# Opening a conditioned decoder layer in other groups of row blocks, with the later conditioning in half rows

## The chip, the cores and the metric

The kernel runs on one core of one Trainium2 chip. The metric is the device time of one execution in microseconds (us); lower is better. The median of three runs stands for a kernel. Beside them one execution was recorded by the hardware profiler; its rows are quoted here and below. Engines are named as in the profile: PE (matmuls), PEld (loads of the stationary operand), DVE (vector), ACT (scalar), POOL (GpSimd), SP (the queue that issues most of the transfers from memory, "DMA").

## The reference, cut to what matters

One layer, 256 tokens, width 2048, everything in float32. A vector `c` conditions all of it: nine vectors of 2048 (shift, scale and gate for each of three sub-layers) come from one product with a large matrix, and the first sub-layer cannot start without its shift and scale.

```python
c_act = jax.nn.silu(c)
mod = (c_act @ w_ada[l] + b_ada[l]).reshape(b, N_MOD, D_MODEL)   # w_ada: 2048 x 18432
h = modulate(rms_norm(x, norm_ffn1[l]), mod[:, 0], mod[:, 1])    # h * (1 + scale) + shift
x = x + 0.5 * mod[:, 2] * swiglu(h, w_ffn1_gu[l], w_ffn1_down[l])
h = modulate(rms_norm(x, norm_mix[l]), mod[:, 3], mod[:, 4])
x = x + mod[:, 5] * token_mixing(h, w_in[l], ...)
h = modulate(rms_norm(x, norm_ffn2[l]), mod[:, 6], mod[:, 7])
x = x + 0.5 * mod[:, 8] * swiglu(h, w_ffn2_gu[l], w_ffn2_down[l])
return rms_norm(x, norm_final)                                   # after the (one) layer
# swiglu: gate, up = split(h @ w_gu); (silu(gate) * up) @ w_down; w_gu is 2048 x 11264
```

## The kernel before, in words

**A product in three parts.** Each matrix product is made from float32 operands that are split into a high part and a rest: ACT casts a weight piece to its high part (`wh`, line 375), DVE subtracts it from the piece and leaves the rest (`wl`, line 377), and PE adds up three products (line 360): high by high (`wh,hh`), high weight by the rest of the activation (`wh,hl`), rest of the weight by high (`wl,hh`). A piece is two row blocks of 128 rows by 512 columns; with the two halves of the tokens it is 2 x 2 x 3 = 12 matmuls of 128x512. The pool `wsp` has three buffers, so ACT can cast a piece only when PE is through with the `wh` products of the piece three earlier. The loads of whole weights go into the pool `raws` (four buffers of 1 MB).

**Conditioning.** The matrix `w_ada` lies transposed in memory. One row of it here is a tile (m, k) of 128x2048 (1 MB): the 128 values k of vector m. A pass (`ada_pass`, line 220) multiplies a part of such a row with silu(c) on DVE and sums it up: a quarter, half or the whole of a row per pass.

**The opening.** The first feed-forward product needs scale (m = 1) and shift (m = 0) for every row block k of its 16, that is 32 rows, 32 MB. So its first 16 column chunks of 512 (8 of the gate, 8 of the up half; `EARLY = 8`) are computed in groups of row blocks: while PE visits all 16 chunks with the row blocks of one group, DVE conditions the row blocks of the next group. The groups are set by `bounds`. Blocks 0 and 1 come in before the groups, with two chunks in whole float32 (line 1099). For each chunk (`visit`) the sum so far has to be carried over from group to group: after a visit ACT copies the two PSUM banks `pa` out to a `part` tile (`to_parts`, line 1219), and before the next visit of that chunk ACT copies the part back into two fresh banks (`open_banks`, line 1191), on which PE adds ("seeding"; the last two chunks of a group stay in PSUM and open the next group). There are four such banks, enough for two visits. In the last group nothing is seeded: `swiglu_up` (lines 705, 706 and 710) adds the parts to the banks on DVE and multiplies gate and up.

**What else fills the opening.** From the group before the last on, the conditioning of the later vectors (`conditioning`, `ROWS_FFN1`) runs beside the products at a rate of one quarter pass per piece (`tick`), 48 passes in the third group and 16 in the last. Its rows go to one half of a slot that the rows of the groups share (`ring`, `alone`), later to buffers of `raws`, and after the opening to a slot with two places of a full row (`two_rows`). The normalised and modulated activations of a pair of row blocks come either from PE transposes (`turned_x`, row blocks under `TURNED`) or from a transposed copy of x that POOL scales (`normed_columns`); ACT modulates them (line 628) and casts them (line 636), DVE subtracts (line 637). The result of the gated chunks is turned over by DMA in steps (`later`, `turn_step`), one step per visit in the last group.

**Order.** The instructions of PE, DVE and ACT are put in order by a scheduler when the program is built, from the order in the code and a model of its own; `tc.issue_after` pins single ones. SP keeps the order of the code. At run time each engine works strictly through its own list, so an instruction that waits holds back all behind it on its engine.

Of the kernel before, what the change touches and what calls it, by code (L numbers as in the profile page):

```python
# [77 lines left out]
def layer_kernel(  # L78
# [138 lines left out]
    def ada_pass(k, w, sums, q, passes=AQ):  # L217

        at = slice(q * D // passes, (q + 1) * D // passes)
        nc.vector.tensor_tensor_reduce(  # L220
            out=w[:, at],
            in0=w[:, at],
            in1=cact[:, at],
            scale=1.0,
            scalar=0.0,
            op0=ALU.mult,
            op1=ALU.add,
            accum_out=sums[:, k, q : q + 1],
        )
# [36 lines left out]
    def conditioning(outputs, place, behind):  # L266
# [4 lines left out]
        step = 0  # L271
        for m, gain, row in outputs:
            sums = own_sums.pop() if own_sums else ada_sums()
            for k in range(KD):
                for q in range(AQ):
                    for i in range(step // AQ, min((step + pace["ahead"]) // AQ + 1, len(tiles))):
                        if i not in held:
                            held[i] = place()
                            ada_load(*tiles[i], held[i])
                    if behind is not None and step < 2 * AQ:  # L280
                        with tc.issue_after(behind.ins):
                            ada_pass(k, held[step // AQ], sums, q)
                    else:
                        ada_pass(k, held[step // AQ], sums, q)
# [348 lines left out]
    def parts_of_h(held, k, h):  # L633

        h = h.rearrange("p (k s) -> p k s", s=S)
        nc.scalar.copy(held.hi[:, k : k + 2, :], h)
        nc.vector.tensor_sub(held.lo[:, k : k + 2, :], h, held.hi[:, k : k + 2, :].bitcast(F32))
# [326 lines left out]
    tiles = [slot(), part[0]]  # L964
    ring = [tiles[0][:, :D], tiles[0][:, D:]]
# [13 lines left out]
    rows_of, alone = {}, [False]  # L979

    def place(m, k):
        if k < 1:
            rows_of[m, k] = raw_row()
        else:
            if not alone[0]:
                ring.reverse()
# [39 lines left out]
    def turned_x(k0):  # L1026

        xn = [t512()[:, : 2 * P] for _ in range(NT)]
        for t in range(NT):
            nc.scalar.mul(xn[t], x_sb[:, t, k0 * P : (k0 + 2) * P], r[:, t : t + 1])  # L1030
        turned = [bank()[:, :S] for _ in range(2)]
        for i in range(2):
# [6 lines left out]
    TURNED = 6  # L1039
# [15 lines left out]
    def normed_columns(k0):  # L1055

        xt = t512()
        both = xt.rearrange("p (k s) -> p k s", s=S)
        nc.sync.dma_start(both, x_t[k0 : k0 + 2].rearrange("k p s -> p k s"))
        nc.gpsimd.tensor_tensor(  # L1060
            out=both, in0=both, in1=root_row[0][:, None, :].broadcast_to([P, 2, S]), op=ALU.mult
        )
        return [xt[:, i * S : (i + 1) * S] for i in range(2)]

    def group(ks, passes=2):

        for k0 in ks[::2]:
            srcs = normed_columns(k0) if k0 >= TURNED else None
            for k in (k0, k0 + 1):
# [699 lines left out]
```

## Time and profile before

| | before |
|---|---|
| median of 3 runs (lowest to highest) | 2356.58 us (2356.07 to 2357.05) |
| the profiled execution | 2357.64 us, its span 2355.5 us |
| PE busy | 2335.7 us (99%) |
| DVE busy | 1673.1 us (71%) |
| ACT busy | 1367.2 us (58%) |
| moved by DMA | 630.24 MB, mean 268 GB/s |
| mean granted PE clock | 0.999 |

The span runs from the first to the last instruction of the profiled execution; what lies around it makes up the rest of its time. "Busy" is the union of an engine's instructions. Matmuls overlap each other in the records, so a group's "mean" is longer than the distance from one matmul to the next. In the timelines a row is a run of like instructions: start, length, engine, line, and in square brackets the idle time before it with what ended it.

### The profile page before, as it was taken

The page shows a single profiled execution, that of the slowest core. Times are in us where ns is not written, and L with a number is a line of the kernel's source. Part 1 is how long each engine was busy: PE and PEld are TensorE (multiplying, and loading weights), DVE is VectorE, ACT ScalarE, POOL GpSimd, SP SyncE. Part 2 cuts the span into 40 slices and gives each one's busy share as a digit, 9 for nine tenths or more (in the row PEclk, how much of TensorE's full clock was granted, in tenths as well). Part 3 has the DMA queues.
Part 4 walks back from the last instruction along what each step waited for, and adds up shares of the span by engine and source line. Part 5 has one row for each costly group of instructions (what it writes and reads, how often), then busy time and mean ns, then how long its engine had stood idle before and what let it go on. Part 6 is the DMA issues. An engine that isn't in the chain of part 4 may idle for free.

```text
span 2355.5 us, 28357 instructions
## 1 busy us (share of the span) xinstructions
PE 2335.7 (99%) x10445; PEld 1918.6 (81%) x10445; DVE 1673.1 (71%) x2576; ACT 1367.2 (58%) x1888; POOL 18.3 (1%) x27
## 2 busy tenths in 40 slices
PE   8999999999999999999999999999999999999998
PEld 5888888888888888778888888888888888888887
DVE  7788888778867768976777776676555555555656
ACT  6766567455556567774556564465455454455544
POOL 0000000000000000000000000000000000000000
PEclk9999999999999999999999999999999999999999
DMA  9989889988765889876778787754767768666553
GB/s 383 375 323 361 355 294 328 336 306 293 302 237 220 293 267 255 258 212 254 267 273 306 288 310 281 272 204 179 259 237 256 242 239 268 223 231 202 193 197 125
DMA packets 191901, 630.24 MB, mean 268 GB/s; under 512 B 113105, under 2 KB 114769, under 8 KB 121233
## 3 DMA queue, kind: packets, MB, share of 16 engines
q1 hardware_dynamic: 189266, 617.41, 74.6%
q0 software_dynamic: 1600, 9.83, 1.0%
q8 instruction: 82, 1.34, 0.2%
q10 hardware_dynamic: 896, 1.19, 0.1%
q14 instruction: 57, 0.47, 0.1%
HBM read 598.47 MB, written 4.22 MB: 256 GB/s over the span
## 4 chain that ended last, share of the span: by engine, by line
PE 96%; DMA 2%; DVE 1%; ACT 1%; issue 0%; SPq 0%; DVEq 0%; ACTq 0%
PE pa L360 93%; DMA raw<-in_w_ffn_gu_dram 1%; DMA rows_x<-in_w_ada_dram 1%; PE ps L1453 0%; DVE slot L220 0%; PE pd L1369 0%; DVE wl L377 0%; ACT wh L375 0%; DMA x_sb<-in_x_dram 0%; PE ps L360 0%; PE pa L1099 0%; PE ps L895 0%; PE pd L1099 0%; DVE rows_x L220 0%; PE ps L1369 0%
## 5 line engine op out<-in xcount | busy, mean ns | idle before, releaser
L377 DVE TENSOR_TENSOR wl<-raw,wh 128x1024 fp32r<-128x1024 f32 x792 | 963.5, 1225 | 511.0 <-ACT wh L375 451.6
L375 ACT CAST wh<-raw 128x1024 fp32r<-128x1024 f32 x792 | 830.6, 1054 | 818.7 <-PE pa L360 752.6
L360 PE MATMUL pa<-wh,hh 128*128 128x512 f32 x2184 | 597.0, 391 | 3.0 <-ACT wh L375 1.7
L360 PE MATMUL pa<-wh,hl 128*128 128x512 f32 x2184 | 592.6, 389 | 0.0
L360 PE MATMUL pa<-wl,hh 128*128 128x512 f32 x2184 | 586.2, 390 | 0.2
L360 PEld LDWEIGHTS pa<-wh,hh 128*128 128x128 f32 x2184 | 407.5, 188 | 91.6 <-ACT wh L375 2.9
L360 PEld LDWEIGHTS pa<-wl,hh 128*128 128x128 f32 x2184 | 409.4, 188 | 86.7 <-DVE wl L377 1.0
L360 PEld LDWEIGHTS pa<-wh,hl 128*128 128x128 f32 x2184 | 409.8, 188 | 86.1 <-issue 0.4
L360 PE MATMUL pa<-wh,a 128*128 128x512 f32 x1824 | 452.1, 389 | 0.0
L360 PEld LDWEIGHTS pa<-wh,a 128*128 128x128 f32 x1824 | 341.7, 188 | 70.6
L360 PE MATMUL pa<-wl,a 128*128 128x512 f32 x912 | 245.1, 389 | 0.0
L220 DVE CUSTOM_DVE_ANT_0 slot<-slot,cact 128x512 f32<-128x512 f32 (+2 forms) x288 | 219.3, 812 | 30.0 <-DMA slot<-in_w_ada_dram 29.5
L360 PEld LDWEIGHTS pa<-wl,a 128*128 128x128 f32 x912 | 171.1, 188 | 35.4
L551 ACT COPY slot<-back 128x512 uint16<-128x512 uint16 x148 | 98.7, 766 | 0.0
L220 DVE CUSTOM_DVE_ANT_0 rows_x<-rows_x,cact 128x512 f32<-128x512 f32 x124 | 78.7, 686 | 18.0 <-DMA rows_x<-in_w_ada_dram 17.8
L410 ACT CAST a<-slot 128x512 fp32r<-128x512 f32 x114 | 70.6, 620 | 29.3 <-PE pa L360 29.0
L535 ACT COPY flat<-t 128x512 uint16<-128x512 uint16 x136 | 76.7, 617 | 8.9 <-DVE t L1526 5.7
L411 DVE TENSOR_TENSOR a<-slot,a 128x512 fp32r<-128x512 f32 x114 | 77.8, 684 | 0.3 <-ACT a L410 0.3
L220 DVE CUSTOM_DVE_ANT_0 raw<-raw,cact 128x512 f32<-128x512 f32 (+1 forms) x92 | 60.7, 709 | 14.6 <-DMA raw<-in_w_ada_dram 14.5
L1219 ACT COPY slot<-pa 128x512 f32<-128x512 f32 x72 | 38.6, 589 | 21.2 <-PE pa L360 21.0
L360 PE MATMUL pa<-wh,home 128*128 128x512 f32 x160 | 39.5, 389 | 0.0
L220 DVE DVE_READ_ACCUMULATOR2_ANT sums<- 128x1 f32 x440 | 35.9, 82 | 0.0
(232 smaller groups left out, 1087.0 us busy)
## 6 DMA issues: line engine op xcount, KB each, us to landing
raw<-in_w_ffn_gu_dram SPq DMA_DIRECT2D x160, 1024.0 KB, 5.5
raw<-in_w_in_dram SPq DMA_DIRECT2D x104, 1024.0 KB, 5.8
raw<-in_w_ffn_down_dram SPq DMA_DIRECT2D x88, 1024.0 KB, 4.9
slot<-in_w_ada_dram SPq DMA_DIRECT2D x87, 1024.0 KB, 7.4
rows_x<-in_w_ada_dram SPq DMA_DIRECT2D x31, 1024.0 KB, 7.1
raw<-in_w_ada_dram SPq DMA_DIRECT2D x22, 1024.0 KB, 5.7
raw<-in_w_swa_branch_dram SPq DMA_DIRECT2D x16, 1024.0 KB, 5.0
raw<-in_w_ret_branch_dram SPq DMA_DIRECT2D x16, 1024.0 KB, 5.4
```

The costliest lines, as they stand in the source:

```text
L220: nc.vector.tensor_tensor_reduce(out=w[:, at], in0=w[:, at], in1=cact[:, at], scale=1.0, scalar=0.0, op0=ALU.mult, op1=ALU.add, accum_out= ...
L360: product = nc.tensor.matmul(banks[t], act[:, j, t * P : (t + 1) * P], weights[:, j, :], start=starts and i == 0 and j == 0, stop=ends and ...
L375: cast.append(nc.scalar.copy(hi, src).ins)
L377: low.append(nc.vector.tensor_sub(lo, src, hi.bitcast(F32)).ins)
L410: nc.scalar.copy(hi, v)
L411: nc.vector.tensor_sub(lo, v, hi.bitcast(F32))
L535: nc.scalar.copy(planes[:, i, :], words(src)[:, :, i])
L551: nc.scalar.copy(into[:, :, :, i], held["turned"][:, i])
L1219: nc.scalar.copy(p, b)
```

## The change

The opening is cut into groups of 2, 3, 4 and 7 row blocks (`bounds = (0, 2, 5, 9, 16)`, before 2, 4, 6 and 4). An odd group ends in a piece of one row block (6 matmuls). `turned_x`, `normed_columns`, `parts_of_h` and `group` take one block or two, and `TURNED` goes from 6 to 5. The rows of the groups get a slot of their own (`rows_home`); `tiles`, the result of the gated chunks, now lies on two of the three `part` slots instead. The conditioning of the later vectors starts with the last group: its 64 passes of the opening are one per piece there (16 visits of four pieces). `two_rows` has four places of half a row, `conditioning` asks for half rows (512 KB) four passes ahead, and this holds for the rest of the kernel. In the second group every third chunk (`by_vector`: 4, 7, 10, 13; chunk 1 is still in PSUM) is not seeded: it starts on fresh banks and DVE adds them to the part afterwards (line 1243 of the changed kernel). In the last group the turning also makes a step in the middle of a visit.

```diff
-    def ada_pass(k, w, sums, q, passes=AQ):
-        at = slice(q * D // passes, (q + 1) * D // passes)
+    def ada_pass(k, w, sums, q, passes=AQ, first=0):
+        n = D // passes
+        at = slice(q * n, (q + 1) * n)
+        here = w[:, (q - first) * n : (q + 1 - first) * n]
...
-        turn = [both[:, :D], both[:, D:]]
+        turn = [both[:, i * D // 2 : (i + 1) * D // 2] for i in range(4)]
...
+        def ask(at):
+            (m, k), q = tiles[at // AQ], at % AQ
+            w = place()
+            n = min(w.shape[1] * AQ // D, AQ - q)
+            w = w[:, : n * D // AQ]
+            c0 = q * D // AQ
+            nc.sync.dma_start(
+                w, w_ada[(m * KD + k) * P : (m * KD + k + 1) * P, c0 : c0 + n * D // AQ]
+            )
+            for i in range(n):
+                held[at + i] = (w, q)
+            return n
...
-                    for i in range(step // AQ, min((step + pace["ahead"]) // AQ + 1, len(tiles))):
-                        if i not in held:
-                            held[i] = place()
-                            ada_load(*tiles[i], held[i])
+                    while asked <= step + pace["ahead"] and asked < AQ * len(tiles):
+                        asked += ask(asked)
+                    w, first = held.pop(step)
...
-    tiles = [slot(), part[0]]
-    ring = [tiles[0][:, :D], tiles[0][:, D:]]
+    tiles = part[:2]
+    rows_home = slot()
+    ring = [rows_home[:, :D], rows_home[:, D:]]
...
-    TURNED = 6
+    TURNED = 5
...
-    bounds = (0, 2, 6, 12, 16)
+    bounds = (0, 2, 5, 9, 16)
...
     def open_banks(n, sums):
         seeded = sums and n in moved
+        if seeded and n in by_vector:
+            added.add(n)
+            seeded = False
...
-        for make, part in prepared.pop(n):
+        for i, (make, part) in enumerate(prepared.pop(n)):
+            if ticks and i == KB // 2:
+                turn_step()
...
     def to_parts(n):
         for p, b in zip(part_of(n), banks.pop(n)):
+            if n in added:
+                with tc.issue_after(low[-1]):
+                    nc.vector.tensor_add(p, p, b)
+                continue
             with tc.issue_after(cast[-1]):
                 nc.scalar.copy(p, b)
...
-        if g == len(groups) - 2:
-            set_pace(ROWS_FFN1, 192, place_early, 0)
+        by_vector = chunks[1::3] if g == 1 else ()
         if final:
-            pace["rate"], pace["ahead"] = 1.0, 1
+            row_ring.append(two_rows(rows_home))
+            set_pace(ROWS_FFN1, 192, place_row, AQ)
...
-            visit(n, ks, n not in stay, g == len(groups) - 2 or final and i < 8, final or (g == len(groups) - 2 and n in stay))
+            visit(n, ks, n not in stay, final, final or (g == len(groups) - 2 and n in stay))
...
-    row_ring.append(two_rows())
```

In the rows of the program's order that follow, `wh_x<-raw_y` is the cast of a piece, `slot<-pa` and `back<-pa` copy a bank out, `pa<-slot` seeds a bank; the last number of a name tells tiles apart.

The first place is the list of ACT in the first group, around the modulation of blocks 2 and 3 (`t<-ps,modc`). Before:

```order
L1219 COPY slot_6_115<-pa_72_353 128x512
L1219 COPY slot_6_115<-pa_73_354 128x512
L628 ACTIVATE t_86_420<-ps_89_425,modc_106 128x256
L628 ACTIVATE t_86_420<-ps_90_426,modc_106 128x256
L1030 ACTIVATE t_122_579<-x_sb_97,rs2_21_150 128x256
L1030 ACTIVATE t_123_580<-x_sb_97,rs2_21_150 128x256
L375 CAST wh_84_401<-raw_81_397 128x1024
L636 CAST hh_3_112<-t_86_420 128x512
L1219 COPY slot_6_115<-pa_77_377 128x512
L1219 COPY slot_6_115<-pa_78_378 128x512
L375 CAST wh_94_443<-raw_91_439 128x1024
```

And in the changed kernel:

```order
L1246 COPY slot_6_115<-pa_82_397 128x512
L1246 COPY slot_6_115<-pa_83_398 128x512
L644 ACTIVATE t_96_464<-ps_99_469,modc_106 128x256
L644 ACTIVATE t_96_464<-ps_100_470,modc_106 128x256
L1047 ACTIVATE t_122_575<-x_sb_97,rs2_21_150 128x128
L1047 ACTIVATE t_123_576<-x_sb_97,rs2_21_150 128x128
L391 CAST wh_94_445<-raw_91_441 128x1024
L653 CAST hh_3_112<-t_96_464 128x512
L1246 COPY slot_6_115<-pa_87_421 128x512
L1246 COPY slot_6_115<-pa_88_422 128x512
L391 CAST wh_104_487<-raw_101_483 128x1024
```

The cast of the piece of the ninth visit (`wh_94`) still stands behind the copies of the visit before, the modulation and the scaling for the next block; that scaling is 128 columns instead of 256, and it comes two visits later than before (before, `wh_84` is the cast of the seventh).

The second place is the list of ACT in the second group, from its fourth visit on. Before (a visit has two pieces of two row blocks; `raw_156` is the fifth visit, `raw_163` the sixth, `raw_170` the seventh):

```order
L375 CAST wh_161_801<-raw_156_774 128x1024
L375 CAST wh_164_819<-raw_163_817 128x1024
L1219 COPY slot_5_114<-pa_152_737 128x512
L1219 COPY slot_5_114<-pa_153_738 128x512
L1191 COPY pa_166_823<-slot_5_114 128x512
L1191 COPY pa_167_824<-slot_5_114 128x512
L375 CAST wh_168_844<-raw_163_817 128x1024
L1219 COPY slot_5_114<-pa_159_780 128x512
L1219 COPY slot_5_114<-pa_160_781 128x512
L375 CAST wh_171_862<-raw_170_860 128x1024
L1191 COPY pa_173_866<-slot_6_115 128x512
L1191 COPY pa_174_867<-slot_6_115 128x512
```

And in the changed kernel (a visit has a piece of two blocks and one of one block; `raw_155` with `pa_158` and `pa_159` is the fifth visit, a chunk whose sum DVE adds; `raw_162` the sixth, `raw_169` the seventh, `raw_176` the eighth, again one for DVE):

```order
L391 CAST wh_167_798<-raw_162_774 128x512
L1246 COPY slot_5_114<-pa_151_711 128x512
L1246 COPY slot_5_114<-pa_152_712 128x512
L1212 COPY pa_165_780<-slot_5_114 128x512
L1212 COPY pa_166_781<-slot_5_114 128x512
L391 CAST wh_170_810<-raw_169_808 128x1024
L1246 COPY slot_5_114<-pa_165_780 128x512
L1212 COPY pa_172_814<-slot_6_115 128x512
L1212 COPY pa_173_815<-slot_6_115 128x512
L391 CAST wh_174_835<-raw_169_808 128x512
L391 CAST wh_177_847<-raw_176_845 128x1024
L1246 COPY slot_5_114<-pa_166_781 128x512
```

Before, each pair of copies out is followed by the seeding of the visit after next. Now the seeds of the seventh visit (`pa_172`, `pa_173`) stand behind the first copy out of the sixth (`slot_5_114<-pa_165`), which needs the sixth visit's sum to be complete.

The third place is the list of ACT a little further on, around the modulation of the next group's blocks (`t<-t,modc`). Before:

```order
L1219 COPY slot_5_114<-pa_160_781 128x512
L375 CAST wh_171_862<-raw_170_860 128x1024
L1191 COPY pa_173_866<-slot_6_115 128x512
L1191 COPY pa_174_867<-slot_6_115 128x512
L628 ACTIVATE t_175_875<-t_146_695,modc_106 128x256 x2
L375 CAST wh_177_900<-raw_170_860 128x1024
L636 CAST hh_3_112<-t_175_875 128x512
L1219 COPY slot_5_114<-pa_166_823 128x512
L1219 COPY slot_5_114<-pa_167_824 128x512
L375 CAST wh_180_918<-raw_179_916 128x1024
L1191 COPY pa_182_922<-slot_6_115 128x512
L1191 COPY pa_183_923<-slot_6_115 128x512
```

And in the changed kernel, where `raw_183` with `pa_186` and `pa_187` is the ninth visit and `raw_190` the tenth:

```order
L391 CAST wh_181_870<-raw_176_845 128x512
L391 CAST wh_184_882<-raw_183_880 128x1024
L391 CAST wh_188_904<-raw_183_880 128x512
L1246 COPY slot_6_115<-pa_172_814 128x512
L644 ACTIVATE t_195_929<-t_145_675,modc_106 128x256 x2
L1246 COPY slot_6_115<-pa_173_815 128x512
L1212 COPY pa_186_886<-slot_6_115 128x512
L653 CAST hh_3_112<-t_195_929 128x512
L391 CAST wh_191_916<-raw_190_914 128x1024
L1212 COPY pa_187_887<-slot_6_115 128x512
L1212 COPY pa_193_920<-slot_6_115 128x512
L1212 COPY pa_194_921<-slot_6_115 128x512
```

Before, the seeds `pa_173` and `pa_174` stand ahead of the modulation, with a full visit to go. Now the modulation, the cast `hh` and the cast of the tenth visit's first piece (`wh_191`) stand between the copies of the seventh visit and the second seed (`pa_187`) of the ninth, and the cast of the ninth's second piece (`wh_188`) stands ahead of them all.

More of the change, by code (lines that the diff above doesn't have):

```diff
@@ L1024, in square, with turned_x @@
         )
-    def turned_x(k0):
-        xn = [t512()[:, : 2 * P] for _ in range(NT)]
+    def turned_x(k0, nk=2):
+        xn = [t512()[:, : nk * P] for _ in range(NT)]
         for t in range(NT):
-            nc.scalar.mul(xn[t], x_sb[:, t, k0 * P : (k0 + 2) * P], r[:, t : t + 1])
-        turned = [bank()[:, :S] for _ in range(2)]
-        for i in range(2):
+            nc.scalar.mul(xn[t], x_sb[:, t, k0 * P : (k0 + nk) * P], r[:, t : t + 1])
+        turned = [bank()[:, :S] for _ in range(nk)]
+        for i in range(nk):
             for t in range(NT):
```

50 lines of the change are left out of this document (23 added, 27 removed).

## The prediction, before the changed kernel was run

> **What bounds the kernel now.** I read the head of the page first, then busy time by stretch of the opening, then PE's own idle time in the timeline, and last the engine that each idle time was waiting for.
>
> ```profile
> span 2355.5 us, 28357 instructions
> PE 2335.7 (99%) x10445; PEld 1918.6 (81%) x10445; DVE 1673.1 (71%) x2576; ACT 1367.2 (58%) x1888; POOL 18.3 (1%) x27
> ```
>
> PE is idle for 2355.5 - 2335.7 = 19.8 us in all; nothing else can be gained unless PE gets less to do. Where it lies (columns: length, then busy time and instructions of PE, PEld, DVE, ACT, POOL, granted clock, DMA share, GB/s):
>
> ```profile
> 0.00:10.00 10.00, 7.48 (x10) 2.90 (x10) 2.91 (x11) 4.51 (x9) 1.82 (x8) 1.00 0.81 297
> 10.00:20.00 10.00, 4.09 (x8) 1.86 (x8) 9.17 (x27) 5.65 (x15) 0.19 (x1) 1.00 1.02 396
> 27.00:67.50 40.50, 38.71 (x170) 30.23 (x169) 34.45 (x39) 30.59 (x49) 0.00 (x0) 1.00 0.98 377
> 67.50:154.50 87.00, 87.00 (x386) 72.03 (x385) 71.63 (x99) 65.28 (x98) 4.58 (x3) 1.00 0.93 367
> 154.50:285.50 131.00, 130.49 (x576) 107.65 (x575) 107.84 (x188) 77.75 (x108) 4.25 (x2) 1.00 0.88 347
> 285.50:372.00 86.50, 86.50 (x384) 71.47 (x383) 76.57 (x119) 60.32 (x82) 2.16 (x4) 1.00 0.87 295
> ...
> 1360.00:1380.00 20.00, 19.19 (x85) 15.57 (x84) 18.31 (x30) 11.87 (x16) 0.00 (x0) 1.00 0.75 221
> 2340.00:2355.50 15.50, 7.26 (x61) 7.06 (x59) 6.63 (x17) 2.04 (x6) 0.00 (x0) 0.87 0.37 136
> ```
>
> The four middle rows are the four groups before the change. The first 20 us lose 2.52 + 5.91 = 8.4 us and the tail 8.2 us; the order of the instructions is the same there before and after. The groups lose 1.79, 0, 0.51 and 0 us, and 0.8 us lie at 1360. So the opening has 2.3 us to give, and 302 us of dense PE work to lose something in.
>
> ```profile
> 45.14 0.60 PE L1034 MATMUL ps<-small_c,t 128*128 128x128 f32 x4
> 46.15 1.21 PE L360 MATMUL pa<-wh,hh 128*128 128x512 f32 x4 [0.41 <-ACT wh L375]
> 48.59 1.19 PE L360 MATMUL pa<-wh,hh 128*128 128x512 f32 x4 [0.30 <-ACT wh L375]
> ...
> 53.49 1.20 PE L360 MATMUL pa<-wh,hh 128*128 128x512 f32 x4 [0.97 <-ACT wh L375]
> ...
> 55.44 1.07 PE L360 MATMUL pa<-wl,hh 128*128 128x512 f32 x4
> 56.35 1.07 PE L360 MATMUL pa<-wh,hh 128*128 128x512 f32 x4
> ```
>
> Four matmuls take 56.35 - 55.44 = 0.907 us, 0.227 each; a visit is 2.72 us with two row blocks, 4.08 with three, 5.44 with four. Each stop costs about 0.13 us more than its idle time (1.20 against 1.07). In all three cases PE waits for a cast, and ACT's own timeline says why the cast is late:
>
> ```profile
> 42.37 1.07 ACT L1219 COPY slot<-pa 128x512 f32<-128x512 f32 x2 [0.75 <-PE pa L360]
> 43.33 1.03 ACT L628 ACTIVATE t<-ps,modc 128x256 f32<-128x256 f32 x2
> 44.24 0.92 ACT L1030 ACTIVATE t<-x_sb,rs 128x256 f32<-128x256 f32 x2
> 45.04 1.05 ACT L375 CAST wh<-raw 128x1024 fp32r<-128x1024 f32 x1
> ...
> 51.42 1.08 ACT L1219 COPY slot<-pa 128x512 f32<-128x512 f32 x2 [2.89 <-PE pa L360]
> 52.38 1.06 ACT L375 CAST wh<-raw 128x1024 fp32r<-128x1024 f32 x1
> ```
>
> ACT works through its list: copies 0.96 (42.37 to 43.33), modulation 0.91, scaling 0.80, then the cast of which 46.15 waits; and at 51.42 two copies that had to wait for PE, then the cast of which 53.49 waits. Added up start to start, the list gives PE's stops to 0.1 us. I use that below: copy pair 0.96, cast of two blocks 0.95, modulation pair about 1.0.
>
> **The change, part by part.** (1) First group, still two blocks a visit. Six rows of 1 MB are conditioned beside it instead of eight, and one modulation burst moves to the ninth visit. There ACT does copies 0.96, modulation 0.91, scaling of 128 columns (I take 0.6, for 0.80 with 256) and a cast 0.95, in all 3.4 us in a visit of 2.72 and some 0.2 of transposes: a stop of about 0.55 us. The others need a list with a cast behind late copies; the new list has most casts ahead of them. 1.79 becomes 0.55: -1.2 us, and -0.4 for three stops fewer. Bounds: 0 (they only move) to -1.8 and -0.4.
>
> (2) Second group, three blocks. Here I see the cost. This is the list in the second group before, with four blocks a visit, and PE beside it:
>
> ```profile
> 85.97 1.05 ACT L375 CAST wh<-raw 128x1024 fp32r<-128x1024 f32 x1 [1.44 <-PE pa L360]
> 86.93 1.07 ACT L1219 COPY slot<-pa 128x512 f32<-128x512 f32 x2
> 87.88 1.12 ACT L1191 COPY pa<-slot 128x512 f32<-128x512 f32 x2
> 88.92 1.06 ACT L375 CAST wh<-raw 128x1024 fp32r<-128x1024 f32 x1
> 91.41 1.05 ACT L375 CAST wh<-raw 128x1024 fp32r<-128x1024 f32 x1 [1.43 <-PE pa L360]
> ```
>
> ```profile
> 83.96 1.07 PE L360 MATMUL pa<-wh,hh 128*128 128x512 f32 x4
> 84.87 1.07 PE L360 MATMUL pa<-wh,hl 128*128 128x512 f32 x4
> ```
>
> Per visit of 5.44 us ACT works 0.95 + 0.96 + 1.04 + 0.95 = 3.9 and waits 1.44. The wait is for a buffer of high parts: the cast starts at 85.97, 2.0 us after the visit began at 83.96, when its `wh` products end (84.87 + 1.07). Whatever stands behind such a cast on ACT starts no sooner. With 4.08 us a visit and the casts 0.95 and about 0.52 (the copies are as long as half a cast), the round is 3.5 us, and a modulation burst adds 1.0 + 0.5. On the average it fits, since four visits lose their copies and seeds to DVE. Along the list it does not, at three places.
> - Sixth visit: the cast of its second piece waits 2.0 us into the fifth, then 0.52, copies 0.96, seeds 1.04: the second seed is there at 4.6, PE wants it at 4.08 + 0.23: 0.3 us.
> - Seventh: its seeds stand behind the first copy out of the sixth, so PE stands still for a copy 0.5, two seeds 1.04, less the 0.23 of the second bank, and 0.2 for the hand-overs: 1.5 us.
> - Ninth: counted from the start of the eighth, the blocked cast is through at 2.0 + 0.5, then copy 0.5, modulation 1.0, copy 0.5, seed 0.5, `hh` 0.5, cast 0.95, second seed 0.5: 7.0 us against 4.08 + 0.23: 2.7 us.
>
> That seeds hold up PE has a row already, in the third group:
>
> ```profile
> 246.93 0.74 PE L360 MATMUL pa<-wh,hh 128*128 128x512 f32 x2 [0.51 <-ACT pa L1191]
> ```
>
> Sum of (2): +4.5 us, in time that PE does not get back. DVE's eight additions (about 0.68 each, the length of the operation on 128x512 in the rows under (3)) each wait for the end of a visit, and the next `wl` stands behind them; the visit that PE is then in, 4.08 us, covers 1.4 for the pair, 1.24 for that `wl` and what is late of a row. So I add nothing for them. Bounds: 0, as in the stretch 67.50:154.50 where ACT has the same kinds of work, and 9 if each of the three is twice as long because DVE's additions or a row come late too.
>
> (3) Third group, four blocks a visit with 14 rows instead of 12 in the second group before. Its nearest row is 67.50:154.50: no idle time, DVE 71.63 of 87. Two rows and half a modulation more on DVE:
>
> ```profile
> L377 DVE TENSOR_TENSOR wl<-raw,wh 128x1024 fp32r<-128x1024 f32 x111 | 136.8, 1244 | 40.8 <-ACT wh L375 40.3
> L220 DVE CUSTOM_DVE_ANT_0 slot<-slot,cact 128x1024 f32<-128x1024 f32 x40 | 47.3, 1219 | 1.7 <-DMA slot<-in_w_ada_dram 1.7
> L220 DVE CUSTOM_DVE_ANT_0 slot<-slot,cact 128x512 f32<-128x512 f32 x48 | 30.4, 686 | 0.6 <-DMA slot<-in_w_ada_dram 0.6
> L710 DVE TENSOR_TENSOR t<-t,slot 128x512 f32<-128x512 f32 x12 | 7.9, 682 | 0.0
> ```
>
> 4 x 1.22 + 0.8 = 5.7 us: 77 of 87. It holds. The old third group with its shared place for rows is gone, and its 0.51 with one stop's 0.13: -0.6 us (bounds 0 and -0.6).
>
> (4) Last group, seven blocks, 42 x 0.227 = 9.52 us a visit. DVE per visit: pieces 3.5 x 1.244 = 4.35, four quarter passes 4 x 0.686 = 2.74, and of the six operations that end a pair of visits (two token halves, three each) half, 3 x 0.682 = 2.05; in all 9.1 us. It fits by 0.4 us. The row nearest to that load is this one, DVE 99% busy and PE without a gap:
>
> ```profile
> 300.00:320.00 20.00, 20.00 (x90) 16.58 (x89) 19.86 (x35) 13.48 (x19) 0.00 (x0) 1.00 0.76 290
> ```
>
> ACT seeds nothing there. The 64 passes cost nothing as long as the 0.4 us hold; if not, the rest of the weight is late next, PE's third of three products.
>
> (5) Half rows: 83 more issues on SP. They wait for a place whose passes ended two passes ago, where a full row waited for the pass just before, with weight loads behind it on SP either way. Outside the opening PE's only stop is the 0.8 us at 1360, so I cost this at nothing (bounds -0.9 and +1). (6) One turned row block fewer, two transposes on PE: 2 x 0.60 / 4, partly overlapped, -0.2 us.
>
> Sum: -1.6 + 4.5 - 0.6 - 0.2 = +2.1 us on the profiled execution's 2357.64 us. That execution is 1.06 us above the median of 2356.58, so I forecast 2356.58 + 2.1 = **2358.7 us**. I count 0.2% (4.7 us) as about what a measurement of this kernel can tell from no change; this is no change by that.
>
> **The rivals.** *A: the second group runs without stops* because ACT gets ahead in the visits that DVE relieves. For it speaks the idle 1.44 us a visit; against it that ACT cannot use it, being held by the buffers and by its order. Then 2356.58 - 2.4 = 2354.2 us.
>
> *B, on the slower side: DVE falls behind in the last group.* Its slack is 0.4 us a visit. DVE stands still when a row of conditioning is late, and every wait of that kind beyond 0.4 us a visit goes to PE:
>
> ```profile
> DVE slot L220 <- DMA slot<-in_w_ada_dram: 19.4, 15, 3.1
> ```
>
> Up to 600 us these waits are 19.4 / 15 = 1.3 us each. One in each of the 16 visits would cost 16 x (1.3 - 0.4) = 14 us, one in every second some 7, on top of the forecast: 2366 us. Against it: in the stretches with the most DVE work these waits sum up to 2.3 us (1.7 and 0.6 above), and half rows are asked for earlier.
>
> *C: the third group is bound by its transfers.* 64 weight blocks of 0.262 MB, 14 rows of 1.049 and 0.9 MB of x are 32.4 MB in 87 us, 372 GB/s. The old second group ran at 367 with PE full, and this row goes well beyond:
>
> ```profile
> 240.00:250.00 10.00, 9.49 (x42) 7.52 (x41) 7.63 (x13) 6.60 (x10) 0.00 (x0) 1.00 1.01 422
> ```
>
> If transfers were held near the 347 GB/s of the old third group as a ceiling, they would take 93 us, 6 us more than PE: 2365 us. The Trainium skill speaks for this rival: its page "DMA: Bandwidth & Descriptors", section Specifications, puts memory at about 358 GB/s for one core; by that the transfers would take an estimated 90.5 us. The trace does not agree: 422 GB/s over 10 us, and 377 over the 40.5 us of the first group.
>
> **How the numbers follow.** The forecast gets 0.58, rival A 0.25, B 0.12, C 0.05. The forecast's own range is 2355.5 to 2362 (its (2) between a third and 1.7 times, the rest as above); some 0.07 of its 0.58 lie over 2361.3. A reaches down to 2353; under 2351.9 I leave 0.03. So faster 0.03, slower 0.07 + 0.12 + 0.05 = 0.24, same 0.73. The range that leaves 2 in 10 out: 2353.5 to 2363.
>
> **What would show it.** In the changed kernel's timeline PE should stop some 20 to 40 us into the second group for `pa<-slot` copies (line 1212), twice for over a microsecond, with a copy out or the modulation ahead on ACT. The first group should show one stop for a cast, the third and last none. I am wrong if the second group is dense, if the last one shows PE waiting for `wl`, or if the rest of the kernel moves by more than a microsecond.

## The result: slower by 0.6%, and not in the opening

| | before | changed |
|---|---|---|
| median of 6 runs (lowest to highest) | 2357.28 us (2356.07 to 2358.11) | 2371.44 us (2364.41 to 2376.51) |
| ratio of the times | | 1.0058, interval 1.0048 to 1.0068 |
| the profiled execution, its span | 2357.64 us, 2355.5 us | 2373.11 us, 2371.3 us |
| PE idle in the span | 19.8 us | 31.1 us |

The forecast was 2358.7 us, in a range up to 2363. The runs of the changed kernel spread over 12 us, those of before over 2. Of the 95 runs of before that stand beside the experiments below, 21 took 2364 to 2371 us at a granted clock of 0.997 or 0.998, against 0.999 in the others (none of the 87 runs of e1 and of e6 to e12 did, and no trace shows why), so medians are compared. The head of the page after:

```profile
span 2371.3 us, 28472 instructions
PE 2340.2 (99%) x10443; PEld 1916.9 (81%) x10443; DVE 1679.0 (71%) x2610; ACT 1363.4 (57%) x1889; POOL 19.4 (1%) x28
```

Busy time by stretch (columns as before: length, PE, PEld, DVE, ACT, POOL, granted clock, DMA share, GB/s). The first four rows are the opening. The last two each lie in a product with a conditioning beside it: from 500 us the one with the down matrix, from 1280 us those of the two branches of the token mixing (SP loads `w_swa_branch` and `w_ret_branch` there):

```profile
40.00:60.00 20.00, 19.25 (x86) 15.31 (x85) 16.72 (x21) 15.30 (x25) 0.00 (x0) 1.00 0.90 327
60.00:120.00 60.00, 59.57 (x263) 49.00 (x262) 47.83 (x68) 44.83 (x72) 3.30 (x2) 1.00 0.92 345
120.00:220.00 100.00, 100.00 (x443) 82.83 (x442) 90.38 (x136) 74.44 (x111) 6.60 (x4) 1.00 0.93 369
220.00:380.00 160.00, 159.28 (x707) 131.69 (x706) 141.38 (x263) 96.83 (x130) 0.54 (x1) 1.00 0.99 338
...
500.00:660.00 160.00, 153.77 (x665) 123.63 (x664) 125.96 (x219) 82.78 (x102) 0.00 (x0) 1.00 0.81 287
...
1280.00:1340.00 60.00, 53.83 (x230) 42.33 (x229) 43.12 (x75) 34.14 (x45) 0.00 (x0) 1.00 0.86 271
```

The same two stretches before:

```profile
500.00:660.00 160.00, 160.00 (x707) 132.55 (x706) 132.01 (x228) 86.97 (x108) 0.00 (x0) 1.00 0.81 305
1280.00:1340.00 60.00, 60.00 (x266) 49.72 (x265) 48.48 (x82) 34.66 (x43) 0.00 (x0) 1.00 0.81 289
```

From 40 us to the end of the groups PE stands still for 0.75 + 0.43 + 0 + 0.72 = 1.9 us, less than the 2.3 us before. The two late stretches have 6.2 us each of idle time, where before has none. The number of matmuls says more than the idle time: before, the same stretches hold 707 and 266, after 665 and 230. That is 78 fewer, at 0.227 us each 17.7 us of work pushed back, more than the whole span grew by (15.8 us). PE's stops by its timeline, first three of the opening's four, then three of the eight in the stretch at 500:

```profile
51.22 1.19 PE L376 MATMUL pa<-wh,hh 128*128 128x512 f32 x4 [0.43 <-ACT wh L391]
53.66 1.20 PE L376 MATMUL pa<-wh,hh 128*128 128x512 f32 x4 [0.33 <-ACT wh L391]
101.56 0.73 PE L376 MATMUL pa<-wh,hh 128*128 128x512 f32 x2 [0.43 <-ACT pa L1212]
...
582.45 1.20 PE L376 MATMUL pa<-wl,a 128*128 128x512 f32 x4 [0.81 <-DVE wl L393]
594.81 1.20 PE L376 MATMUL pa<-wl,a 128*128 128x512 f32 x4 [1.05 <-DVE wl L393]
...
635.35 1.17 PE L376 MATMUL pa<-wh,a 128*128 128x512 f32 x4 [1.63 <-DVE t L660]
```

In all eight stops of that stretch PE waits for DVE. What DVE waits for (us in sum, times, longest, over the whole run) is the conditioning's rows. In the changed kernel:

```profile
DVE slot L222 <- DMA slot<-in_w_ada_dram: 101.0, 67, 4.2
DVE rows_x L222 <- DMA rows_x<-in_w_ada_dram: 77.5, 50, 3.3
```

And before, 47.3 us in all where it is 178.5 now:

```profile
DVE slot L220 <- DMA slot<-in_w_ada_dram: 29.5, 24, 3.1
DVE rows_x L220 <- DMA rows_x<-in_w_ada_dram: 17.8, 15, 3.2
```

**A loop that is too short for the transfer.** SP's and DVE's timelines around the stop at 594.81 show how these waits keep themselves going. First SP, which sends the loads of whole weights and of half rows:

```profile
584.17 0.33 SPq L367 DMA_DIRECT2D raw<-in_w_ffn_down_dram  x1
584.54 0.43 SPq L282 DMA_DIRECT2D slot<-in_w_ada_dram  x1
590.03 0.33 SPq L367 DMA_DIRECT2D raw<-in_w_ffn_down_dram  x1
590.41 0.43 SPq L282 DMA_DIRECT2D slot<-in_w_ada_dram  x1
596.52 0.33 SPq L367 DMA_DIRECT2D raw<-in_w_ffn_down_dram  x1
```

And DVE:

```profile
582.92 1.22 DVE L393 TENSOR_TENSOR wl<-raw,wh 128x1024 fp32r<-128x1024 f32 x1
585.82 0.69 DVE L222 CUSTOM_DVE_ANT_0 slot<-slot,cact 128x512 f32<-128x512 f32 x1 [1.68 <-DMA slot<-in_w_ada_dram]
...
587.05 1.22 DVE L393 TENSOR_TENSOR wl<-raw,wh 128x1024 fp32r<-128x1024 f32 x1
...
588.79 1.22 DVE L393 TENSOR_TENSOR wl<-raw,wh 128x1024 fp32r<-128x1024 f32 x1
592.30 0.69 DVE L222 CUSTOM_DVE_ANT_0 slot<-slot,cact 128x512 f32<-128x512 f32 x1 [2.30 <-DMA slot<-in_w_ada_dram]
...
593.53 1.22 DVE L393 TENSOR_TENSOR wl<-raw,wh 128x1024 fp32r<-128x1024 f32 x1
...
595.27 1.22 DVE L393 TENSOR_TENSOR wl<-raw,wh 128x1024 fp32r<-128x1024 f32 x1
```

A weight load goes out when DVE's second `wl` of an older weight frees its buffer: 582.92 + 1.22 = 584.14 and the load at 584.17, 588.79 + 1.22 = 590.01 and the load at 590.03, 595.27 + 1.22 = 596.49 and the load at 596.52. The half row goes out just behind it. The half of 584.54 is what the pass at 592.30 waits for, 7.8 us later; behind that pass stand the two `wl` of the next weight, whose end lets the next load go. Between the ask and the pass there is only one weight on DVE: at PE's pace 24 matmuls of 0.227 us, 5.44 us, for a transfer that takes about 7. The distance from load to load becomes 5.86 and 6.49 us instead of 5.44, and PE, which needs a weight every 5.44 us, stops.

**Why one weight.** That distance stands in the program's order. For each row or half row asked for between the 60th and the 300th load of a whole weight, I counted how many weights lie between the weight load ahead of its ask on SP and the weight whose `wl` stands ahead of its first pass on DVE. "Three ahead" is the case above: the load of a weight, and the passes already behind the `wl` of the weight three before it.

| passes stand ... of their ask's weight | before | changed |
|---|---|---|
| three ahead | 3 of 86 | 87 of 161 |
| two ahead | 60 | 47 |
| one ahead or level | 23 | 27 |

In both stretches in which PE loses time, three ahead is the rule: 25 of 30 half rows from 500 to 660 us, all 10 from 1280 to 1340. From 380 to 500 us it is 8 of 25; there DVE waits 24.8 us for rows and PE has no gap. Three ahead is not enough by itself: from 1340 to 1400 us it is 8 of 9, DVE waits 9.7 us, and PE has no gap there either.

So the scheduler that orders DVE puts the passes of half rows one weight earlier, as if half a row landed sooner; that this is its reason was not tested. On the chip half the size lands hardly sooner (median us from issue to landing in the last column). Before:

```profile
slot<-in_w_ada_dram SPq DMA_DIRECT2D x87, 1024.0 KB, 7.4
rows_x<-in_w_ada_dram SPq DMA_DIRECT2D x31, 1024.0 KB, 7.1
```

After:

```profile
slot<-in_w_ada_dram SPq DMA_DIRECT2D x132, 512.0 KB, 6.9
rows_x<-in_w_ada_dram SPq DMA_DIRECT2D x62, 512.0 KB, 6.3
```

At two ahead there are two weights, 10.9 us, for 7.4 us; at three ahead 5.44 us for 6.9. This is theory L (the place in DVE's list). The rivals: S, that the smaller transfers themselves cost the time; T, that the code asks too late; and G, that the new groups of the opening and the later start of the conditioning do it.

### The profile page after: what moved, and what is told of

It is laid out like the page before. It is cut to its first block, busy times and chain, and to the rows that moved or that the text cites. A ratio compares the mean times of both kernels' runs of the same rounds, so it can differ in the third digit from the quotient of the medians.

```text
span 2371.3 us, 28472 instructions
## 1 busy us (share of the span) xinstructions
PE 2340.2 (99%) x10443; PEld 1916.9 (81%) x10443; DVE 1679.0 (71%) x2610; ACT 1363.4 (57%) x1889; POOL 19.4 (1%) x28
## 4 chain that ended last, share of the span: by engine, by line
PE 92%; DMA 4%; DVE 3%; issue 1%; ACT 0%; SPq 0%; DVEq 0%; ACTq 0%
PE pa L376 89%; DMA slot<-in_w_ada_dram 2%; DVE wl L393 1%; DMA rows_x<-in_w_ada_dram 1%; DVE slot L222 0%; PE ps L1473 0%; PE pd L1389 0%; DMA x_sb<-in_x_dram 0%; DVE a L427 0%; PE ps L376 0%; PE pa L1117 0%; PE ps L912 0%; PE pd L1117 0%; PE pd L1571 0%; DVE rows_x L222 0%
## 5 line engine op out<-in xcount | busy, mean ns | idle before, releaser
L391 ACT CAST wh<-raw 128x1024 fp32r<-128x1024 f32 (+1 forms) x808 | 833.8, 1037 | 822.4 <-PE pa L376 767.3
L393 DVE TENSOR_TENSOR wl<-raw,wh 128x1024 fp32r<-128x1024 f32 (+1 forms) x808 | 965.0, 1203 | 391.9 <-ACT wh L391 331.7
L222 DVE CUSTOM_DVE_ANT_0 slot<-slot,cact 128x512 f32<-128x512 f32 (+2 forms) x310 | 237.0, 802 | 101.4 <-DMA slot<-in_w_ada_dram 101.0
L222 DVE CUSTOM_DVE_ANT_0 raw<-raw,cact 128x512 f32<-128x512 f32 (+1 forms) x72 | 48.0, 718 | 16.6 <-DMA raw<-in_w_ada_dram 16.3
```

What stands on the lines that cost most here:

```text
L222: nc.vector.tensor_tensor_reduce(out=here, in0=here, in1=cact[:, at], scale=1.0, scalar=0.0, op0=ALU.mult, op1=ALU.add, accum_out=sums[:, ...
L391: cast.append(nc.scalar.copy(hi, src).ins)
L393: low.append(nc.vector.tensor_sub(lo, src, hi.bitcast(F32)).ins)
```

## The experiments

All ratios are to the kernel before, run on the same chip beside it; the chip is not the same in all rows.

| | what | median us (lowest to highest) | ratio, interval | DVE's waits for `slot` + `rows_x`, us |
|---|---|---|---|---|
| e1 | full rows, rest as changed | 2355.28 (2354.14 to 2355.90) | 0.9986, 0.9977 to 0.9996 | 33 |
| e2 | half rows alone | 2373.61 (2368.34 to 2385.47) | 1.0082, 1.0055 to 1.0109 | 173 |
| e3 | passes held in code order | 2368.10 (2365.14 to 2370.34) | 1.0046, 1.0034 to 1.0059 | 2 |
| e4 | full places, two half loads | 2361.31 (2359.24 to 2363.71) | 1.0013, 1.0001 to 1.0025 | 143 |
| e5 | asked half a row earlier | 2373.11 (2367.88 to 2377.88) | 1.0049, 1.0033 to 1.0065 | 161 |
| e6 | held at 8 | 2355.78 (2355.50 to 2356.18) | 0.9979, 0.9965 to 0.9993 | 11 |
| e7 | held at 7 | 2354.99 (2354.84 to 2355.39) | 0.9981, 0.9969 to 0.9993 | 4 |
| e8 | held at 6 | 2355.47 (2355.04 to 2357.16) | 0.9983, 0.9970 to 0.9995 | 7 |
| e9 | held at 4 | 2356.12 (2355.58 to 2356.92) | 0.9984, 0.9971 to 0.9997 | 3 |
| e10 | full rows, held at 7 | 2355.31 (2355.06 to 2355.61) | 0.9984, 0.9973 to 0.9994 | 1 |
| e11 | e7, second group all on ACT | 2354.37 (2353.93 to 2354.70) | 0.9979, 0.9969 to 0.9989 | 4 |
| e12 | e1, second group all on ACT | 2354.80 (2353.74 to 2356.87) | 0.9982, 0.9972 to 0.9992 | 35 |

**e1 and e2: which half of the change.** e1 is the changed kernel with two places of a full row:

```diff
-        turn = [both[:, i * D // 2 : (i + 1) * D // 2] for i in range(4)]
+        turn = [both[:, :D], both[:, D:]]
```

> The changed kernel with its two places of a full row (1 MB) instead of four of half a row; groups, the rows' own slot, the added chunks and the stepped turning stay. Theory L (the list): what costs time is where the half rows' passes stand in DVE's list. The scheduler counts a half row as landing sooner and puts its passes one weight tile earlier, while from issue to landing a half takes 6.9 us and a full row 7.0 to 7.4. Theory S (the size): transfers of 512 KB are worked off less well, so all transfers are later. Theory G (the groups): the loss comes from the groups and the later start of the conditioning. L and S: 2355 to 2358 us, DVE's waits for rows after the opening back from 101 and 78 us to about 30 and 18. G: about 2371 us.

e2 is the kernel before with `ada_pass`, `two_rows` and `conditioning` of the changed one and nothing else:

```diff
-        turn = [both[:, :D], both[:, D:]]
+        turn = [both[:, i * D // 2 : (i + 1) * D // 2] for i in range(4)]
...
+                    while asked <= step + pace["ahead"] and asked < AQ * len(tiles):
+                        asked += ask(asked)
```

> The kernel before with nothing changed but the half rows: four places of half a row after the opening and loads asked for by halves; groups 2, 4, 6, 4 as before. L and S: 2365 to 2373 us, with PE's stops between 500 and 660 us and near 1300 us as in the changed kernel. G: 2357 us.

The half rows are the whole loss, and G falls: without them the changed kernel is 0.1% below before, with them alone the old one is slower. Their price is 2371.44 - 2355.28 = 16.2 us on the changed kernel and 2373.61 - 2356.89 = 16.7 us on the old one; this second price is rough, since e2's four runs lie 17 us apart (by the interval of its ratio 13 to 26 us). In the same two stretches PE has no gap in e1. By the count above, 2 of e1's 89 rows have their passes three ahead, and 81 of e2's 148.

**e3: passes not before their place in the code.**

```diff
                     else:
-                        ada_pass(k, w, sums, q, first=first)
+                        with tc.issue_after(low[-1]):
+                            ada_pass(k, w, sums, q, first=first)
```

> The changed kernel, half rows and all, with each conditioning pass held in DVE's list behind the weight piece at which the code has it (by the order list a half row's first pass then stands two weight tiles behind the tile that its load follows on SP, where it stood three tiles ahead of it). Same transfers, same sizes, same arithmetic. L: 2354 to 2358 us, DVE's waits for rows under 15 us. S: the transfers are as slow as before, so weights and rows stay late: 2363 us or more. G: about 2371 us.

Half of L held: DVE's waits for rows are gone but for 2.2 us. The time is not back, which L had not expected; by the time alone S, with its 2363 us or more, fits this run. What waits now is ACT, for the weights (us in sum, times, longest; the first of these rows is 7.1 us in 2 waits in the changed kernel):

```profile
ACT wh L392 <- DMA raw<-in_w_in_dram: 57.3, 19, 5.1
ACT wh L392 <- DMA raw<-in_w_ffn_gu_dram: 54.6, 20, 5.4
ACT wh L392 <- DMA raw<-in_w_ffn_down_dram: 40.9, 17, 4.0
```

And SP waits at the ask for a half row (L282) until a place is free, that is, until the passes on the half four before it are through:

```profile
SPq L282 <- DVE sums L222: 539.0, 142, 8.0
```

In this run the passes stand mostly two weights behind the ask's weight (119 of 161). The places come free so late that SP, which keeps the order of the code, holds back the weight loads behind the ask. A pass can be too early in DVE's list, or too late for SP. The first side costs 16 us here, the second 13 (2368.10 - 2355.28). Not all of the 13 is waiting: in e3's trace PE stands still for 1.51 us before 521.55 and for 2.48 us before 525.23, and the eight matmuls from 525.23 take 3.78 us, where the eight from 517.16 took 1.98. The granted clock from 525 to 530 us is 0.50. The twelve matmuls from 525.23 to 530.51 us take an estimated 2.6 us more than 12 x 0.227.

**e4: the same half transfers in places of a full row**, two asked for together:

```diff
-        turn = [both[:, i * D // 2 : (i + 1) * D // 2] for i in range(4)]
+        turn = [both[:, :D], both[:, D:]]
...
-            nc.sync.dma_start(
-                w, w_ada[(m * KD + k) * P : (m * KD + k + 1) * P, c0 : c0 + n * D // AQ]
-            )
+            src = w_ada[(m * KD + k) * P : (m * KD + k + 1) * P, c0 : c0 + n * D // AQ]
+            for i in range(0, n, 2):
+                cs = slice(i * D // AQ, (i + 2) * D // AQ)
+                nc.sync.dma_start(w[:, cs], src[:, cs])
```

> The changed kernel with two places of a full row, each row fetched by two loads of 512 KB that are asked for together. The sizes of transfers are those of the changed kernel, the time of asking that of full rows; in the order list most first passes stand two weight tiles ahead, a third of them three. L: between the two, 2357 to 2364 us. S: 2368 to 2374 us. G: about 2371 us.

2361.3 us is 10 us less than the changed kernel with transfers of the same size, against S. Here 30 of 178 half rows have their passes three ahead, 117 two ahead, and the loss is in between too. By itself this left room for a share of S; e6 to e9 do not.

**e5: ask earlier.**

```diff
-            set_pace(ROWS_FFN1, 192, place_row, AQ)
+            set_pace(ROWS_FFN1, 192, place_row, AQ + 2)
```

(and the same at the three other places that set it)

> The changed kernel with every half row asked for six passes ahead instead of four (half a row sooner on SP; the places stay four, so an ask waits for a place whose passes end just before). DVE's list is not moved by this: most first passes of a half still stand three weight tiles ahead of the weight tile behind which the half was issued. Theory L (the scheduler counts a half row as landed sooner than it is and puts its passes one weight tile too early in DVE's list): the scheduler follows the ask, the distance in the list stays, so no gain: 2367 to 2374 us, DVE's waits for rows again 120 to 190 us in sum. Rival T (half rows are simply asked for too late by the code): half a row sooner takes most of the waits away: 2355 to 2360 us, waits for rows under 60 us.

```profile
DVE slot L222 <- DMA slot<-in_w_ada_dram: 81.0, 63, 3.5
DVE rows_x L222 <- DMA rows_x<-in_w_ada_dram: 80.4, 50, 3.7
```

T falls as stated: asking earlier in the code changes nothing that counts, because the passes follow the ask in the list (82 of 160 still three ahead).

**e6 to e9: the same transfers, asks and places; only DVE's list moves.** Each pass is held behind the `wl` of a piece some pieces back (eight pieces are two weights):

```diff
                     else:
-                        ada_pass(k, w, sums, q, first=first)
+                        with tc.issue_after(low[-8]):      # e7: -7, e8: -6, e9: -4
+                            ada_pass(k, w, sums, q, first=first)
...
-        del low[:-1]
+        del low[:-16]
```

> The changed kernel with each pass after the opening's first two rows of conditioning held on DVE behind the high-part subtraction eight pieces (two weight tiles) before its place in the code: the half transfers, their places and SP's order are unchanged, only DVE's list moves; most first passes of a half now stand one or two weight tiles ahead of the tile behind which the half was issued, against three in the changed kernel. Theory L: DVE's waits for rows fall from 178 us in sum to under 60, SP still gets its places in time, and the kernel comes to 2355 to 2361 us. Rival S (the half transfers themselves cost the time) or T (asked for too late): 2366 to 2373 us, with the waits on DVE where they were.

> As the run before, held behind the seventh piece back: nearly all first passes stand one weight tile ahead, none three. Theory L: 2355 to 2360 us, waits for rows under 25 us in sum; if the best place in the list lies between DVE waiting for rows and SP waiting for places, this is at or near it. Rivals S and T: 2366 to 2373 us.

> As before, held behind the sixth piece back: first passes one tile ahead or level with the weight tile of the ask, so a place comes free half a weight tile later than in the run before. Theory L with its other side (places free too late, weight loads queued behind the ask on SP): no waits of DVE for rows, the first waits for weights come back, 2357 to 2364 us, between the run before and the one with passes in code order (2368). Rivals S and T: no different from the changed kernel, 2366 to 2373 us.

> As the runs with held passes, held behind the fourth piece back (one weight tile before the code's place): first passes of a half level with the weight tile of its ask or one behind it. It looks for the far edge, where the place of a half comes free so late that SP stands still for it with the weight loads behind it. If that edge is gradual: 2357 to 2363 us, ACT waiting for weights (raw) 40 to 100 us in sum outside the opening. If it is a step at the code's own place (two behind, 2368 us): 2355 to 2356 us as held at six. Rivals S and T: 2366 to 2373 us.

| passes stand ... of their ask's weight | changed | e6 | e7 | e8 | e9 | e3 |
|---|---|---|---|---|---|---|
| three ahead | 87 | 0 | 0 | 0 | 0 | 0 |
| two ahead | 47 | 76 | 20 | 10 | 0 | 0 |
| one ahead | 26 | 80 | 130 | 92 | 17 | 1 |
| level | 1 | 5 | 7 | 55 | 86 | 1 |
| one behind | 0 | 0 | 4 | 4 | 54 | 30 |
| two or more behind | 0 | 0 | 0 | 0 | 4 | 129 |
| median us | 2371.4 | 2355.8 | 2355.0 | 2355.5 | 2356.1 | 2368.1 |

This settles it: all 16 us come back when no pass stands three ahead, with 512 KB transfers as before (they land in 6.8 and 6.2 us in e7, hardly sooner than in the changed kernel). S and T expected no difference. The passes' own rows in e7 (last column: idle time of DVE ahead of them, nearly all for rows) and the two late stretches:

```profile
L222 DVE CUSTOM_DVE_ANT_0 slot<-slot,cact 128x512 f32<-128x512 f32 (+2 forms) x310 | 243.0, 800 | 3.4 <-DMA slot<-in_w_ada_dram 3.2
L222 DVE CUSTOM_DVE_ANT_0 rows_x<-rows_x,cact 128x512 f32<-128x512 f32 x124 | 84.9, 686 | 0.4 <-DMA rows_x<-in_w_ada_dram 0.4
```

```profile
500.00:660.00 160.00, 160.00 (x708) 132.48 (x707) 132.78 (x229) 87.18 (x107) 0.00 (x0) 1.00 0.86 301
...
1280.00:1340.00 60.00, 60.00 (x267) 49.67 (x266) 49.56 (x83) 34.73 (x42) 0.00 (x0) 1.00 0.86 293
```

The other edge came out other than I expected for e8 (2357 to 2364 us). SP waits long for places in e9 already, and no loss shows:

```profile
SPq L282 <- DVE sums L222: 395.5, 115, 7.5
```

From two ahead to one behind, the time stays within 1.2 us; at two behind (e3) it is 12 us more. That is nearer to e9's second case, a step (2355 to 2356 us expected, 2356.1 measured), than to its first. Where between e9 and e3 the time turns was not tried.

**e10: the full rows held too** (e1's edit with e7's):

```diff
-        turn = [both[:, i * D // 2 : (i + 1) * D // 2] for i in range(4)]
+        turn = [both[:, :D], both[:, D:]]
...
+                        with tc.issue_after(low[-7]):
+                            ada_pass(k, w, sums, q, first=first)
```

> Full rows again (two places of a full row) and, as in the run held at seven, each pass behind the seventh piece back. Theory L prices a wait of DVE only where PE runs out of work: the full rows' 50 us of waits on DVE reached PE in no window after the opening, so taking them away gains nothing that counts: 2354.5 to 2356 us, waits for rows under 20 us in sum. If those waits still cost something, 2353 to 2354.5 us. If a full place now comes free too late, over 2357 us.

As expected: e1's 33 us of waits for rows are gone and the time is the same. These waits on DVE had no price that the times show; those of the changed kernel had one where PE ran out of work. With the passes in place, halves (e7) and full rows (e10) are within 0.4 us.

**e11 and e12: my costing of the second group.** They take DVE's additions out, so that ACT copies and seeds every chunk, on e7 and on e1:

```diff
-        by_vector = chunks[1::3] if g == 1 else ()
+        by_vector = ()
```

> The run held at seven with the second group's four relieved chunks seeded and copied out by ACT again like the others (the tuple of chunks is empty), so DVE's eight additions go and ACT has 3.5 us of work in each visit of 4.08. Prediction's way of costing (ACT's list added up against visits in order): PE stops around the modulation of each pair of blocks, 1.5 to 4 us more than in the run held at seven: 2356.5 to 2359 us. Against it (PE's own list has half a visit of other banks to work on meanwhile, and the places of high parts bind, not the list): no more than 0.5 us in the stretch from 60 to 120 us, 2354.8 to 2355.6 us.

> The changed kernel with full rows in two places, no pass held, and the second group's copies and seeds all on ACT (the two edits that gained, together). If the two are independent: 2355.3 less the 0.6 us that the last run gained over the one held at seven, 2354.4 to 2354.9 us, with the second group dense; the stop of 1.3 us near 376 us of the held runs is absent and 0.5 us lie near 1350 us instead. If the additions' gain belonged to the held passes: 2355 to 2356 us.

e11's second group, with 51.1 us of ACT's work in 60 instead of 44.7:

```profile
60.00:120.00 60.00, 60.00 (x266) 49.70 (x265) 46.09 (x66) 51.10 (x86) 3.42 (x2) 1.00 0.92 356
```

Dense. The way of costing that put 4.5 us here fails where ACT has more to do, too. When the relief by DVE goes, so does the stop at about 101 us (0.48 us in e7). e11 is 0.6 us under e7, and lower than either expectation; e12 is 0.5 us under e1, as expected if the two edits are independent. Both pairs ran on different chips and their intervals against before overlap: the traces show this gain, the times alone do not. The two medians are the lowest of the study, 0.2% below before, but by the ratios e11 and e12 can't be told from e6 to e10.

## Why the prediction was wrong, point by point

- **(5) half rows "at nothing (bounds -0.9 and +1)"**: this step failed, and it measured +16.2 us (e1). I weighed SP (more issues, 95 by the trace and not the 83 I gave; places free sooner) and PE's stops outside the opening, of which there was one. I did not ask where the passes go in DVE's list when the transfer's size changes, although the order of the changed kernel shows it: 87 of 161 first passes three weights ahead instead of 3 of 86. What I cited for cover was that PE does not stop there before. It was cover for the old distance of 10.9 us, not for one of 5.44.
- **(2) second group +4.5 us**: measured 0.43 us, one stop. The mechanism was right in one place: PE waits at 101.56 for a `pa<-slot` copy behind the modulation. The size was wrong, since I added up ACT's list only and let PE want the second bank 0.23 us after the first, as in the rows of before, where four matmuls of a kind alternate between the banks. In the changed kernel's second group PE's list finishes one bank (`pa_165`), then the other (`pa_166`). PE in the sixth visit (2, 2, 2, 1, 1, 1 matmuls for each bank):

```profile
88.72 0.62 PE L376 MATMUL pa<-wh,hh 128*128 128x512 f32 x2
...
90.53 0.39 PE L376 MATMUL pa<-wl,hh 128*128 128x512 f32 x1
90.76 0.62 PE L376 MATMUL pa<-wh,hh 128*128 128x512 f32 x2
...
92.57 0.39 PE L376 MATMUL pa<-wl,hh 128*128 128x512 f32 x1
92.80 0.62 PE L376 MATMUL pa<-wh,hh 128*128 128x512 f32 x2
```

  and ACT beside it:

```profile
91.01 0.59 ACT L1246 COPY slot<-pa 128x512 f32<-128x512 f32 x1 [1.23 <-PE pa L376]
91.63 1.11 ACT L1212 COPY pa<-slot 128x512 f32<-128x512 f32 x2
...
100.44 0.57 ACT L1246 COPY slot<-pa 128x512 f32<-128x512 f32 x1
100.91 0.59 ACT L1212 COPY pa<-slot 128x512 f32<-128x512 f32 x1
```

  The first bank is complete at 90.76, its copy starts at 91.01, the two seeds follow, and PE is busy with the second bank until 92.80. So the seventh visit's 1.5 us are covered by those 2.04 us, the sixth's 0.3 likewise. In the ninth visit the second seed is due 2.04 us after the first, not 0.23, and PE waits for the first alone: by my list that one is there at 2.0 + 0.5 + 0.5 + 1.0 + 0.5 + 0.5 = 5.0 us against 4.08, 0.9 us late. The trace has 0.43 (the copy at 100.91, PE at 101.56). I had PE's order at hand and read ACT's alone.
- **(1) first group -1.6**: two stops of 0.43 and 0.33 us instead of one of 0.55; 1.79 became 0.76, for -1.2 forecast -1.0. The size is right, the number of stops is not.
- **(3) third group -0.6**: dense from 120 to 220 us, at 369 GB/s. Right, and rival C did not occur. For that rival the Trainium skill's page "DMA: Bandwidth & Descriptors", section Specifications, gave about 358 GB/s for one core; this stretch again lies above it with PE full.
- **(4) last group 0**: 0.72 us at its end, at 375.6 us (none in e1), none inside. Nearly right.
- **(6) two transposes -0.2**: too small to be told apart.
- **The sum without (5)**: e1 against before on its chip, 2355.28 - 2356.89 = -1.6 us, where (1) to (4) and (6) gave +2.1. With (2) at 0.43 and its restart of 0.13 they give -1.8.
- **The rivals**: A's time (2354.2) is close to e1's, and what it foresaw, a second group almost without stops, is what happened. Its reason, that DVE's relief lets ACT get ahead, did not hold: without the relief (e11, e12) the group is dense. B had the right chain (a late row, DVE stands still, `wl` behind it, PE's third product late) in the wrong place: I bounded it in the last group of the opening, and dismissed it since "half rows are asked for earlier". The loss came where the passes stand one weight behind such an ask, at 500 and 1280 us. The last sentence of "what would show it" named the rest of the kernel moving by over a microsecond as a way to be wrong; it was the one that came.

## What to carry to other kernels

Where a scheduler sets an engine's order, the size of a transfer is also an input to that order: after any change of a load, measure in the built order the distance between its issue and its first user, in units of the loop's period, and hold it against the landing time in the trace, queue included. Pin the consumer where the distance is under the landing time; here one `issue_after` was worth 16 us, and the usable room was wide (two weights ahead to one behind). When an engine's list is added up to find a stop, add up the list of the engine that waits as well: what it has left to do between two needs is the cover.

## What the runs showed that I had not expected

- Half the bytes land hardly sooner when they are queued right behind a 1 MB load: 512 KB in 6.9 us, 1 MB in 7.4 (medians). The Trainium skill's page "DMA: Bandwidth & Descriptors", section "Anatomy of one DMA — SWDGE (gpsimd) path", fits about 2.0 us and the bytes at 436 GB/s for a single transfer; an estimate by it is 3.2 us for 512 KB, 4.4 for 1 MB. The trace does not agree, in size or in difference; but the page fits transfers that GpSimd issues, and these are issued by SP behind others, so this is no test of its fit.
- The landing time is not the transfer's own. In e3, where the half rows go out when a place is free, the same 512 KB land in 5.4 (`slot`) and 5.1 us (`rows_x`).
- The held kernel is steady: e7's eleven runs lie within 0.6 us, where the changed kernel's six lie within 12 and the 32 of before on e7's chip within 14. That the waits on transfers make the spread is not shown: e1, with 33 us of them, stays within 1.8.
